# The normed input of a two-layer encoder moved by 32 bytes in its partitions

## The chip, the cores and the metric

The kernel runs on one core of a Trainium2 chip. The metric is the device time of one execution in microseconds (us); the time of a kernel is the median of several executions. In the profile the engines are PE (TensorE's matmuls), PEld (TensorE's loading of the stationary operand), DVE (VectorE), ACT (ScalarE), POOL (GpSimd) and SP (SyncE, which issues most DMAs).

## The reference

The kernel computes a small two-layer encoder for 256 tokens of width 2048 in float32, with 256 memory tokens beside them:

```python
m = rms_norm(mem, mem_norm)
h = x
for i in range(2):
    n = rms_norm(h, attn_norm[i])
    z = n @ (a_w_in if i == 0 else b_w_in)          # queries, keys, values, memory queries
    mix = neighbourhood_attention(...) if i == 0 else gqa_block_attention(...)
    km, vm = split(m @ w_mem_kv[i])
    cross = memory_attention(qm, km, vm)
    h = h + concatenate([mix, cross]) @ w_o[i]
    n = rms_norm(h, mlp_norm[i])
    h = h + square(relu(n @ w_up[i])) @ w_down[i]   # inner width 8192
return rms_norm(h, final_norm)
```

## The kernel before

**Split numbers.** Every float32 operand of a large product is split in two parts of a type that TensorE multiplies at full rate: hi, a rounded copy (ScalarE, line 299), and lo, the rest (VectorE, line 300). A product is then three matmuls: hi·hi, hi·lo and lo·hi. The activations lie split in SBUF; the weights stream from memory in chunks of 1 MB (128 partitions of 2048 floats), are split in halves of 1024 columns, and are used once.

**Operands.** In each matmul one operand moves through the array (512 or 256 columns here) and the other is stationary (128 columns); the profile writes out<-moving,stationary or the other way round, whichever the program names first. Four helpers issue nearly all matmuls:

- `m_products` (lines 205, 208, 209): the weights (hi, lo, or uh, ul, or th, tl) move with 512 columns, a block of 128 tokens of the activations (nT, memT, cat or a_p) is stationary. It forms the values, the second layer's whole input projection, the output projections and the last eighth of the MLP's second product.
- `s_products` (lines 218 and 221): 128 columns of the weights are stationary, the activations (memT or nT) move, 512 columns with hi and 256 with lo, two of each in turn. It forms the memory keys and the first layer's queries and keys.
- `u_products` (lines 670 to 672): the MLP's first product; the weights uh and ul are stationary, hT moves with 256 columns.
- the second product's `run` (lines 779 to 781): the weights (bh, bl, then th, tl) move with 512 columns, a_s is stationary; the products are named p1 to p7, by the sums and differences of a seven-product scheme.

**Order.** The memory's keys and values come first, then the first layer's input projection with its attention beside it, its output projection and its MLP, and the same for the second layer. In the MLP, 56 times per layer, 48 matmuls of ps_u alternate with 21 of p (9 with bh and bl, 12 with th and tl). A hand-made list of steps, each with loading, preparing and running parts, sets the order on all engines; data that an engine waits for is prepared some steps ahead.

**Where the tiles lie.** Tiles are taken from pools, and pools are stacked in each partition of SBUF: const, keep and small on the left, behind them ring and cat (in the attention stages) or mlp (in the MLP); on the right, from the other end downwards, work (attention) or side (MLP). Tiles and pools are rounded to 32 bytes and not further. `wide` (line 418) takes a tile of 32768 bytes in keep, which holds four things in turn: nT0, the first layer's normed input (taken in `x_norm`, line 531); hT0, the MLP's input (in `guard`, line 605); nT1, the second layer's normed input (in `down_done`, line 917); hT1; at the end a row of gains (line 899). In the program before it begins at byte 34464, which is 32 past a multiple of 64 (and of 128). Counted from the sizes, the others begin at:

| tiles | pool | bytes past a multiple of 128 |
|---|---|---|
| nT0, hT0, nT1, hT1 | keep, tag wide | 32 |
| raw, hi, lo | ring | 0 |
| memT, cat | cat | 0 |
| z, c, a_s, a_p, bh, bl, th, tl | mlp | 0 |
| raw_U, uh, ul, b, t, raw_T | side | 96 |
| qT, kT, km, sc, pT, va, vb, vm | work | 96 |

Slices of these tiles begin at whole multiples of 64 bytes from the tile's start (512 bytes for 128 columns).

Of the kernel before, what the change touches and what calls it, by code (L numbers as in the profile page):

```python
# [11 lines left out]
F32R = mybir.dt.float32r  # L12
# [5 lines left out]
P = 128  # L18
# [3 lines left out]
KT = D // P  # L22
# [48 lines left out]
def encoder_kernel(ctx: ExitStack, tc: tile.TileContext, t: dict, out: bass.AP):  # L71
# [4 lines left out]
    def opened(name, side="left", space=None, bufs=1):  # L76
        kw = {"space": space} if space else {}
        manager = tc.tile_pool(name=name, bufs=bufs, side=side, reuse_waits="tile", **kw)
        pools[name] = manager, manager.__enter__()
        return pools[name][1]  # L80

    def closed(*names):
        for name in names:
            pools.pop(name)[0].__exit__(None, None, None)

    const = opened("const")
    keep = opened("keep")
# [11 lines left out]
    def open_ring():  # L99
        at.ring = opened("ring")  # L100
        at.cat = opened("cat")
# [84 lines left out]
    def later(n, fn, *args):  # L186
        pending.append((state["tick"] + n, fn, args))
# [133 lines left out]
    def split_pair(dst, src, which, k):  # L321

        g = gain(which, k)
        nc.scalar.activation(dst[:, k, :SEQ], src, AF.Copy, scale=g)
        nc.vector.scalar_tensor_tensor(dst[:, k, SEQ:], src, g, dst[:, k, :SEQ].bitcast(F32),  # L325
                                       op0=ALU.mult, op1=ALU.subtract)
# [88 lines left out]
    def get(name):  # L415
        return lambda: box[name]

    def wide(name):
        return keep.tile([P, KT, 512], F32R, tag="wide", name=name)

    def keys(name):
        return at.work.tile([P, NMH, 512], F32R, tag="keys", bufs=1, name=name)
# [105 lines left out]

    def x_norm(j):
        if j == 0:  # L530
            box["nT"] = wide("nT0")
        for k in (2 * j, 2 * j + 1):
            split_pair(box["nT"], box["xT"][k // 8][:, k % 8, :], G_A0, k)

# [49 lines left out]
    def sum_squares(which, i, nb):  # L584
        sq = at.side.tile([P, 512], BF16, tag="junk", bufs=2, name="sq")
        nc.scalar.activation(sq, h[:, i, nb * 512 : (nb + 1) * 512], AF.Square,
                             accum_out=ssq[which][:, i, nb : nb + 1])

    def mean_square(which, n, name):

        s = small.tile([P, NT], F32, tag="ss0", name="ss_t")
        nc.vector.tensor_reduce(s, ssq[which][:, :, :n], axis=AX.X, op=ALU.add)
        v = keep.tile([P, NT], F32, tag=name, name=name)
        nc.vector.tensor_scalar(v, s, 1.0 / (n * 512), EPS, op0=ALU.mult, op1=ALU.add)
        return v

    def o_done(layer, nb):
        which = 2 * layer

        def guard():  # L600

            box["near"] = mean_square(which, GUARD, "near")
            box["scale"] = keep.tile([P, NT], F32, tag="scale", name="scale")
            nc.gpsimd.tensor_tensor(box["scale"], box["near"], mhalf[:, :NT], op=ALU.pow)
            box["hT"] = wide(f"hT{layer}")
# [195 lines left out]
    def add_scaled(hs, src, factor):  # L801
        nc.vector.scalar_tensor_tensor(hs, src, factor, hs, op0=ALU.mult, op1=ALU.add)
# [104 lines left out]
    def down_done(layer, nb):  # L907
        def f(w):
            for i in range(NT):
                add_scaled(h[:, i, nb * 512 : (nb + 1) * 512], w.ps[i], box["inv"][:, i : i + 1])  # L910
            for i in range(NT):
                sum_squares(2 * layer + 1, i, nb)
            if layer == 1:
                later(1, times_gf, nb)
                return
            if nb == 0:
                box["nT"] = wide("nT1")
            later(1, transposed, box["nT"], lambda i, k: h[:, i, k * P : (k + 1) * P],
                  list(range(nb * 4, nb * 4 + 4)), G_A1)
            if nb == 3:  # L920
                closed("mlp")
                open_ring()

                def norm():
                    box["rstd"] = keep.tile([P, NT], F32, name="rstd1")
                    v = mean_square(1, 4, "full")
                    nc.gpsimd.tensor_tensor(box["rstd"], v, mhalf[:, :NT], op=ALU.pow)
                later(2, norm)
        return f
# [145 lines left out]
    for j in range(8):  # L1075
        later(24 + j, x_norm, j)
# [122 lines left out]
```

## Time and profile before

| | |
|---|---|
| median of 3 executions | 2070.88 us (2068.25 to 2073.3) |
| the profiled execution | 2069.22 us |
| its span, first to last instruction | 2067.2 us |
| mean granted TensorE clock | 0.997 of full speed |
| ACT busy | 1251.3 us (61%) |
| DMA | 433.78 MB, 210 GB/s on average |

The span is what the page's shares refer to; the profiled execution's time has some 2 us around it. The page lists the busy time of each engine, then the chain of work that ended last, then the costliest groups of instructions with the mean duration of one. Durations of matmuls overlap, since one begins before the one before has drained, so a row's mean is no rate: rates come from start times, in the timeline or in the windows view, which gives busy time, instruction counts (those still running at the stretch's start included), clock and DMA share for chosen stretches of the span.

### The profile page before, as it was taken

The page shows a single profiled execution, that of the slowest core. Times are in us where ns is not written, and L with a number is a line of the kernel's source. Part 1 is how long each engine was busy: PE and PEld are TensorE (multiplying, and loading weights), DVE is VectorE, ACT ScalarE, POOL GpSimd, SP SyncE. Part 2 cuts the span into 40 slices and gives each one's busy share as a digit, 9 for nine tenths or more (in the row PEclk, how much of TensorE's full clock was granted, in tenths as well). Part 3 has the DMA queues.
Part 4 walks back from the last instruction along what each step waited for, and adds up shares of the span by engine and source line. Part 5 has one row for each costly group of instructions (what it writes and reads, how often), then busy time and mean ns, then how long its engine had stood idle before and what let it go on. Part 6 is the DMA issues. An engine that isn't in the chain of part 4 may idle for free.

```text
span 2067.2 us, 31544 instructions
## 1 busy us (share of the span) xinstructions
PE 2039.7 (99%) x12516; PEld 1815.0 (88%) x12516; DVE 1668.6 (81%) x2047; ACT 1251.3 (61%) x1642; POOL 119.2 (6%) x144
## 2 busy tenths in 40 slices
PE   8999999999999999999999999999999999999998
PEld 6888888889999999999988888889999999999996
DVE  6767667566899999999996667666988999999896
ACT  6755555555666666666656557555666666666653
POOL 0000000000010000010000001000000000000000
PEclk9999999999999999999999999999999999999999
DMA  7755555736777787787765454536877787777773
GB/s 266 297 183 177 189 175 170 274 105 202 223 235 231 218 240 225 225 240 226 231 201 209 171 177 143 188 138 197 232 227 227 224 242 222 233 232 223 232 225 121
DMA packets 92996, 433.78 MB, mean 210 GB/s; under 512 B 10416, under 2 KB 12080, under 8 KB 59568
## 3 DMA queue, kind: packets, MB, share of 16 engines
q1 hardware_dynamic: 75456, 399.25, 57.3%
q0 software_dynamic: 16816, 31.46, 8.6%
q8 instruction: 98, 1.61, 0.3%
q10 hardware_dynamic: 576, 1.05, 0.1%
q14 instruction: 50, 0.41, 0.1%
HBM read 398.17 MB, written 4.19 MB: 195 GB/s over the span
## 4 chain that ended last, share of the span: by engine, by line
PE 97%; DVE 1%; issue 1%; DMA 1%; ACT 0%; SPq 0%; POOLq 0%; POOL 0%; DVEq 0%; ACTq 0%
PE ps_u L672 11%; PE ps_u L670 11%; PE ps_u L671 11%; PE p L779 9%; PE p L780 9%; PE p L781 9%; PE ps_m L205 8%; PE ps_m L208 8%; PE ps_m L209 8%; PE ps_s L218 7%; PE ps_s L221 3%; PE pt_a L379 1%; PE pt_n L317 0%; PE av L387 0%; PE sc_ps L353 0%
## 5 line engine op out<-in xcount | busy, mean ns | idle before, releaser
L671 PE MATMUL ps_u<-hT,uh 128*128 128x256 f32 x2048 | 569.3, 278 | 3.7 <-DVE hT L325 3.6
L670 PE MATMUL ps_u<-hT,uh 128*128 128x256 f32 x2048 | 569.9, 278 | 1.5 <-ACT uh L299 1.5
L672 PE MATMUL ps_u<-hT,ul 128*128 128x256 f32 x2048 | 569.3, 278 | 1.5 <-DVE ul L300 1.3
L299 ACT ACTIVATE uh<-raw_U 128x1024 fp32r<-128x1024 f32 x278 | 295.0, 1062 | 325.2 <-PE ps_u L671 301.9
L300 DVE TENSOR_TENSOR lo<-raw,hi 128x1024 fp32r<-128x1024 f32 (+1 forms) x222 | 266.3, 1204 | 167.7 <-ACT hi L299 166.4
L671 PEld LDWEIGHTS ps_u<-hT,uh 128*128 128x128 f32 x2048 | 385.9, 188 | 9.1 <-DVE hT L325 4.5
L670 PEld LDWEIGHTS ps_u<-hT,uh 128*128 128x128 f32 x2048 | 386.3, 189 | 7.6 <-ACT uh L299 1.9
L672 PEld LDWEIGHTS ps_u<-hT,ul 128*128 128x128 f32 x2048 | 387.1, 189 | 3.0 <-DVE ul L300 2.3
L300 DVE TENSOR_TENSOR ul<-raw_U,uh 128x1024 fp32r<-128x1024 f32 x278 | 337.9, 1219 | 35.4 <-ACT uh L299 35.4
L299 ACT ACTIVATE hi<-raw 128x1024 fp32r<-128x1024 f32 (+1 forms) x222 | 231.3, 1047 | 218.7 <-PE ps_m L209 116.1
L299 ACT ACTIVATE th<-t 128x2048 fp32r<-128x2048 f32 x112 | 215.2, 1921 | 124.9 <-PE p L781 118.2
L300 DVE TENSOR_TENSOR tl<-t,th 128x2048 fp32r<-128x2048 f32 x112 | 256.3, 2288 | 40.3 <-ACT th L299 39.9
L300 DVE TENSOR_TENSOR bl<-b,bh 128x1536 fp32r<-128x1536 f32 x112 | 196.1, 1751 | 0.4
L780 PE MATMUL p<-tl,a_s 128*128 128x512 f32 x448 | 177.2, 396 | 0.0
L781 PE MATMUL p<-th,a_s 128*128 128x512 f32 x448 | 174.4, 389 | 0.0
L299 ACT ACTIVATE bh<-b 128x1536 fp32r<-128x1536 f32 x112 | 166.2, 1484 | 6.4
L779 PE MATMUL p<-th,a_s 128*128 128x512 f32 x448 | 166.1, 395 | 0.0
L759 POOL DMA_DIRECT2D t<-b x112 | 97.0, 866 | 1168.3 <-DVE t L758 377.5
L218 PE MATMUL ps_s<-nT,hi 128*128 128x512 f32 x448 | 141.7, 394 | 0.0
L781 PE MATMUL p<-bh,a_s 128*128 128x512 f32 x336 | 131.1, 390 | 0.0
L780 PE MATMUL p<-bl,a_s 128*128 128x512 f32 x336 | 130.9, 390 | 0.0
L758 DVE TENSOR_TENSOR t<-t,b 128x512 f32<-128x512 f32 x112 | 77.2, 690 | 48.2 <-DMA t<-in_w_pair 36.4
(235 smaller groups left out, 3510.6 us busy)
## 6 DMA issues: line engine op xcount, KB each, us to landing
raw_U<-in_w_up SPq DMA_DIRECT2D x128, 1024.0 KB, 6.6
b<-in_w_pair SPq DMA_DIRECT2D x112, 768.0 KB, 4.5
raw<-in_w_o SPq DMA_DIRECT2D x32, 1024.0 KB, 5.0
t<-in_w_pair SPq DMA_DIRECT2D x112, 256.0 KB, 3.4
t<-b POOLq DMA_DIRECT2D x112, 256.0 KB, 6.6
raw<-in_w_b SPq DMA_DIRECT2D x21, 1024.0 KB, 5.0
raw<-in_w_av SPq DMA_DIRECT2D x12, 1024.0 KB, 4.9
raw<-in_w_aq SPq DMA_DIRECT2D x12, 1024.0 KB, 4.9
```

Of the source, the lines that this page charges most:

```text
L205: first = nc.tensor.matmul(w.ps[i], ah, hi[:, s], start=st, stop=False)
L208: nc.tensor.matmul(w.ps[i], ah, lo[:, s], start=False, stop=False)
L209: nc.tensor.matmul(w.ps[i], al, hi[:, s], start=False, stop=sp)
L218: nc.tensor.matmul(ps, hi[:, s], acts[:, k0 + j, :], start=k0 + j == 0, stop=False)
L299: nc.scalar.activation(dst_hi, src, AF.Copy)
L300: nc.vector.tensor_tensor(dst_lo, src, dst_hi.bitcast(F32), op=ALU.subtract)
L670: nc.tensor.matmul(ps, hi[:, s], acts[:, k, :SEQ], start=k == 0, stop=False)
L671: nc.tensor.matmul(ps, hi[:, s], acts[:, k, SEQ:], start=False, stop=False)
L672: nc.tensor.matmul(ps, lo[:, s], acts[:, k, :SEQ], start=False, stop=k == KT - 1)
L779: nc.tensor.matmul(ps, a[:, 0, ai, :], hi[:, s], start=begins, stop=False)
L780: nc.tensor.matmul(ps, a[:, 0, ai, :], lo[:, s], start=False, stop=False)
L781: nc.tensor.matmul(ps, a[:, 1, ai, :], hi[:, s], start=False, stop=ends)
```

## The change

`wide` gets a parameter, shift. Its tile now has room for 8 more floats (32800 bytes in place of 32768), and what it returns is a view of the old size that begins `shift` floats into it. The two normed inputs nT0 and nT1 ask for a shift of 8 floats, 32 bytes; hT0 and hT1 ask for none. So nT begins at byte 34496, a multiple of 64, and hT at 34464 as before.

```diff
-    def wide(name):
-        return keep.tile([P, KT, 512], F32R, tag="wide", name=name)
+    def wide(name, shift=0):
+        room = keep.tile([P, KT * 512 + 8], F32R, tag="wide", name=name)
+        return room[:, shift : shift + KT * 512].rearrange("p (a b) -> p a b", b=512)
...
     def x_norm(j):
         if j == 0:
-            box["nT"] = wide("nT0")
+            box["nT"] = wide("nT0", 8)
...
             if nb == 0:
-                box["nT"] = wide("nT1")
+                box["nT"] = wide("nT1", 8)
```

The tile itself is 32 bytes longer, and the left pools are stacked behind it.

## The prediction

> **What bounds the kernel now.** I read the page first: the span, the busy times and the chain that ended last.
>
> ```profile
> span 2067.2 us, 31544 instructions
> ...
> PE 2039.7 (99%) x12516; PEld 1815.0 (88%) x12516; DVE 1668.6 (81%) x2047; ACT 1251.3 (61%) x1642; POOL 119.2 (6%) x144
> ...
> PE 97%; DVE 1%; issue 1%; DMA 1%; ACT 0%; SPq 0%; POOLq 0%; POOL 0%; DVEq 0%; ACTq 0%
> PE ps_u L672 11%; PE ps_u L670 11%; PE ps_u L671 11%; PE p L779 9%; PE p L780 9%; PE p L781 9%; PE ps_m L205 8%; PE ps_m L208 8%; PE ps_m L209 8%; PE ps_s L218 7%; PE ps_s L221 3%; PE pt_a L379 1%; PE pt_n L317 0%; PE av L387 0%; PE sc_ps L353 0%
> ```
>
> TensorE is busy for 99% of the span and is 97% of the chain. So the time is the sum of the intervals from one matmul's start to the next, and a change of addresses counts if it changes such an interval. A matmul's duration in the trace (388 ns) is latency, since they overlap; the interval must be taken from starts. So next the timeline, in two stretches that run the same code (line 205 to 209, moving tile hi or lo) with different stationary tiles.
>
> ```profile
> 392.24 0.39 PE L208 MATMUL ps_m<-lo,cat 128*128 128x512 f32 x1
> ...
> 395.87 0.39 PE L205 MATMUL ps_m<-hi,cat 128*128 128x512 f32 x1
> ```
>
> ```profile
> 1238.08 0.40 PE L208 MATMUL ps_m<-lo,nT 128*128 128x512 f32 x1
> ...
> 1241.81 0.40 PE L209 MATMUL ps_m<-hi,nT 128*128 128x512 f32 x1
> ```
>
> Both have 16 steps. With cat a step takes 3.63/16 = 226.9 ns, with nT 3.73/16 = 233.1 ns. Shape, moving tile and line are the same; the stationary tile's address is not: cat begins at a multiple of 64 bytes, nT 32 past one. Below I call the first **even** and the second **odd**. The windows view gives such stretches for every pair of kinds, and its clock column shows 1.00 in all of them, so no throttle explains them. Columns: stretch, length, busy time and matmuls begun or still running, clock, DMA share, GB/s.
>
> ```profile
> core 0: us, PE busy (x), PEclk, DMA share, GB/s
> 392.24:395.87 3.63, 3.63 (x17) 1.00 1.01 414
> 1238.08:1241.81 3.73, 3.73 (x18) 1.00 0.37 154
> 1076.75:1079.56 2.81, 2.81 (x14) 1.00 0.25 105
> 1125.80:1127.40 1.60, 1.60 (x8) 1.00 1.00 420
> 1307.26:1308.94 1.68, 1.68 (x17) 1.00 0.63 190
> 529.33:531.60 2.27, 2.27 (x23) 1.00 1.00 325
> 717.11:719.58 2.47, 2.47 (x23) 1.00 0.96 232
> 518.32:523.79 5.47, 5.47 (x49) 1.00 0.59 218
> 523.79:528.62 4.83, 4.83 (x24) 1.00 0.77 202
> 158.25:158.94 0.69, 0.69 (x6) 1.00 0.71 297
> ```
>
> Steps counted in the timeline as above, the rows from the third on give:
> - uh with a_p, odd moving and even stationary, 512 columns: 12 steps, 2.81/12 = 234.2 ns.
> - uh with nT, both odd, 512 columns: 7 steps, 228.6 ns.
> - attention scores and values (sc_ps, av), both odd, 256 columns: 14 steps, 120.0 ns.
> - ps_u (hT with uh), both odd, 256 columns: 20 steps, 113.5 ns; in another group 21 steps, 117.6 ns.
> - a whole MLP group of 48 ps_u: 5.47 us, 114.0 ns each. The group of 21 p behind it (both even, 512 columns): 4.83 us, 230.0 ns each, so above the 226.9 of cat: after each change of kind the intervals take some ten matmuls to come down.
> - four ps_s with nT (two of 512 columns, two of 256): 0.69 us.
>
> Thus mixed parity costs 6 to 7 ns per matmul, both even nothing, and both odd anything from nothing (113.5 = half of 226.9) to 6.5 ns (120.0). The DMA share goes from 0.25 to 1.01 and does not order them.
>
> At this place the Trainium skill, "TensorE: Matmul & The Clock Gate", section "Step-by-step: what each phase is for", speaks against any effect: TensorE has two independent SBUF read ports, one for the moving and one for the stationary operand. The trace does not bear that out as far as speed goes (226.9 against 233.1 ns); by the rule the sum would be nothing.
>
> **What the change does, part by part.** No instruction, DMA, wait or queue is added or moved. It moves addresses, and more than it names. nT becomes even. The tile of tag wide grows by 32 bytes, though, and all that is allocated behind it on the left side (small, then ring with raw, hi, lo and cat with memT and cat, or mlp with bh, bl, th, tl, a_s, a_p, c, z) moves 32 bytes with it: even becomes odd. hT stays odd, and the right side (work, side: uh, ul, raw_U, t, qT, kT) stays odd.
>
> ACT, DVE and the DMAs first. ACT and DVE already do the same work to odd and even tiles:
>
> ```profile
> L299 ACT ACTIVATE uh<-raw_U x278: 1042/1062/1069, 391.6 to 2040.6; 128x1024 fp32r<-128x1024 f32 x139
> L299 ACT ACTIVATE hi<-raw x222: 614/1061/1222, 6.4 to 1372.0; 128x1024 fp32r<-128x1024 f32 x107, 128x512 fp32r<-128x512 f32 x4
> ```
>
> ```profile
> L300 DVE TENSOR_TENSOR ul<-raw_U,uh x278: 1209/1218/1227, 392.9 to 2041.7; 128x1024 fp32r<-128x1024 f32 x139
> L300 DVE TENSOR_TENSOR lo<-raw,hi x222: 682/1225/1227, 7.0 to 1373.2; 128x1024 fp32r<-128x1024 f32 x107, 128x512 fp32r<-128x512 f32 x4
> ```
>
> Medians (middle number) 1062 odd against 1061 even, and 1218 against 1225: nothing. What hides a small change of theirs is slack on DVE, as 17 alternations of the MLP (ps_u and p groups) show; the columns are the stretch, its length and the busy times of PE, PEld, DVE, ACT and POOL:
>
> ```profile
> 520.73:695.83 175.10, 175.10 (x1175) 160.17 (x1174) 159.11 (x170) 115.36 (x118) 14.80 (x17) 1.00 0.78 229
> ```
>
> DVE works 159.11 of 175.10 us. If its operations became over 10% longer that cover would be gone, and each alternation would last as long as DVE's work.
>
> The TensorE counts come from the source view (count behind each x; two moving, hi and lo, make three matmuls per product, so the rows of line 205 stand for three times as many):
>
> ```profile
> L205 PE MATMUL ps_m<-hi,nT x264: 389/396/486, 125.1 to 1273.0; 128*128 128x512 f32 x132
> L205 PE MATMUL ps_m<-hi,cat x256: 387/389/501, 350.4 to 1382.6; 128*128 128x512 f32 x128
> L205 PE MATMUL ps_m<-hi,memT x64: 387/389/397, 31.7 to 100.6; 128*128 128x512 f32 x64
> L205 PE MATMUL ps_m<-uh,a_p x64: 388/396/502, 1074.0 to 2055.1; 128*128 128x512 f32 x64
> L205 PE MATMUL ps_m<-th,a_p x64: 387/389/398, 1080.7 to 2057.9; 128*128 128x512 f32 x64
> L205 PE MATMUL ps_m<-uh,nT x24: 387/394/399, 1117.1 to 1147.7; 128*128 128x512 f32 x24
> ```
>
> ```profile
> L779 PE MATMUL p<-th,a_s x448: 389/395/401, 503.2 to 2010.5; 128*128 128x512 f32 x150
> L779 PE MATMUL p<-bh,a_s x336: 387/389/401, 498.4 to 2000.7; 128*128 128x512 f32 x168
> ```
>
> ```profile
> L218 PE MATMUL ps_s<-nT,hi x448: 389/392/582, 101.3 to 349.9; 128*128 128x512 f32 x150
> ```
>
> One price is unknown: both odd at 512 columns in long rows. Its bounds are 226.9 ns (as ps_u at 113.5 has it) and 226.9 + 6.5 = 233.4 ns (the 6.5 that scores and values pay). Between lies 228.6, uh with nT, from 7 steps of a stage with 72 matmuls. I take **233.4**: the scores and values at 120.0 have both tiles at one offset (96 past a multiple of 128), as the moved tiles will have (32 past on both sides), whereas the fast ps_u pairs hT, 32 past, with uh, 96 past, and so does uh with nT. That is the choice on which the sign hangs.
>
> 1. hi with nT, 264 × 3 = 792: mixed before, mixed after (233.1 to 234.2 at most): 0, bounds 0 and 792 × 1.1 = 0.9 us.
> 2. uh with nT, 72: both odd to mixed, 72 × (234.2 − 228.6) = +0.4 us.
> 3. ps_s with nT, 448 × 2 = 896, groups of four: mixed before and after. 0; bounds from 4 clean ones (2 × 226.9 + 2 × 113.5 = 681 ns) to 707 ns, which adds to each of the four the 4.1 that ps_u pays in its slow groups: 224 × −9 to 224 × +17 ns, −2.0 to +3.8 us.
> 4. cat 768, memT 192, th with a_p 192, in all 1152, both even to both odd: 1152 × 6.5 = 7.5 us; a tenth of them follow a change of kind and are not clean today, so **+6.7**; bounds 0 and 7.5.
> 5. p, 112 × 21 = 2352, both even to both odd: 21 × 233.4 = 4.90 for 4.83 us, 112 × 0.07 = **+8.0**; lower bound 21 × 226.9 = 4.76, −7.8 us.
> 6. ps_u keeps its addresses, 48 per alternation. Clean it is 48 × 113.5 = 5.45, so 0.02 of its 5.47 is coming down after p. Behind a p of its own parity this may go, at most 112 × 0.02 = −2.4 us; I take half, −1.2.
> 7. uh with a_p, 192: mixed to both odd, by uh with nT: 192 × (228.6 − 234.2) = −1.1 us.
>
> Sum: 0.4 + 6.7 + 8.0 − 1.2 − 1.1 = +12.8 us. The profiled execution took 2069.22 us (the span 2067.2 and 2.0 around it), so 2082.0; it lies 1.7 below the median of 2070.88. On the median that is 2083.7, and I say 2083. Within the bounds of items 3 to 6 this forecast alone goes from 2076 to 2089.
>
> **The rivals.**
> *Equal parity is what counts* (faster). Both odd is as clean as both even, and a group that follows one of its own parity starts clean. Then an alternation is 48 × 113.5 + 21 × 226.9 = 10.21 us in place of 175.10/17 = 10.30: −0.09 × 112 = −10 us; uh with a_p gives 192 × −7.3 = −1.4, uh with nT +0.4. That is 2060. It decides if p behind ps_u runs at 227 from its first matmuls. For it speaks ps_u at 113.5; against it speak scores and values at 120.0, and the 117.6 that ps_u has at times. 0.15.
>
> *Both odd costs what uh with nT costs*, 228.6: p 21 × 228.6 = 4.80, −0.03 × 112 = −3.4; item 4 1152 × 1.7 × 0.9 = +1.8; items 2, 6 and 7 stay; −3.5, so 2067. For it: the only row of that shape. Against: seven steps. 0.13.
>
> *ps_u falls into its slow state behind the changed p.* It has the addresses it had, but 117.6 in some groups shows that what runs before decides. 48 × (117.6 − 113.5) = 0.20 us × 112 = +22 on top: 2105, or 2090 on the rival before. For it: the changed p no longer settles. Against: most groups of today come down behind a p of 230.0 on average. 0.12.
>
> *Addresses count for nothing and the difference between cat and nT has another cause*, such as what DMA writes meanwhile (shares 1.01 and 0.37, the slower one having less): 2071. 0.10. It is also what the Trainium skill, "SBUF — State Buffer", section "Specifications (TRN2)", suggests: 16-byte cachelines, of which 32 bytes are two whole ones; on that figure an estimate of the change is nothing, and the two stretches above do not agree with it.
>
> *The change does no more than it says* (what lies behind is rounded back to 64): only nT gets even. 792 × (226.9 − 233.1) = −4.9, ps_s −2.0, uh with nT +0.4: 2064. 0.05.
>
> **How the numbers follow.** The forecast has 0.45. The range 2058 to 2095 holds it and all rivals but the slow ps_u at 2105. A measurement of this kernel tells about 0.2%, 4.1 us, from no change. Faster: the first rival, the last, and some of the second, 0.23. Same: the rest of the second and the fourth, 0.20. Slower: forecast and slow ps_u, 0.57.
>
> **What would show it.** The same instructions in the same order, clock 1.00. In the timeline: hi with cat at 233 (item 4), not 227; p groups of 4.90 us, not 4.83 (item 5); ps_u groups no longer than 5.47, or 5.64 if the third rival is right; hi with nT still 233, which says that hi moved; uh with a_p below 234. Cat at 227 and p at 4.76 would mean that equal parity counts and I have the wrong sign; hi with nT at 227 and cat at 227 that nothing but nT moved.

## The result

| | before | changed |
|---|---|---|
| median of 6 executions | 2069.9 us (2068.25 to 2073.3) | 2083.41 us (2081.07 to 2088.6) |
| ratio to before, 95% interval | | 1.0064 (1.0054 to 1.0074) |
| profiled execution's span | 2067.2 us | 2081.0 us |

The changed kernel is 13.5 us slower. Its page, the span, the busy times and the end of the chain of waits:

```profile
span 2081.0 us, 31544 instructions
...
PE 2053.4 (99%) x12516; PEld 1833.4 (88%) x12516; DVE 1670.8 (80%) x2047; ACT 1249.8 (60%) x1642; POOL 119.2 (6%) x144
...
PE 97%; DVE 1%; issue 1%; DMA 1%; ACT 0%; SPq 0%; POOLq 0%; POOL 0%; DVEq 0%; ACTq 0%
PE ps_u L673 12%; PE ps_u L671 11%; PE ps_u L672 11%; PE p L780 9%; PE p L781 9%; PE p L782 9%; PE ps_m L205 8%; PE ps_m L208 8%; PE ps_m L209 8%; PE ps_s L218 6%; PE ps_s L221 3%; PE pt_a L379 1%; PE pt_n L317 0%; PE sc_ps L354 0%; PE av L387 0%
```

The counts are those of before, and TensorE still has 97% of the chain. ACT and DVE are within 3 us of before. Only ps_u has a larger share. The windows view of TensorE in the changed kernel, with stretches like those of before: one group of 48 ps_u, the 21 p behind it, 17 such alternations, 16 steps of hi with cat, 16 of hi with nT (stretch, length, busy time and matmuls, clock, DMA share, GB/s):

```profile
518.05:523.70 5.65, 5.65 (x49) 1.00 0.50 190
523.70:528.49 4.79, 4.79 (x24) 1.00 0.90 230
518.05:695.53 177.48, 177.48 (x1175) 1.00 0.77 226
391.16:394.79 3.63, 3.63 (x18) 1.00 1.00 409
1244.07:1247.79 3.72, 3.72 (x17) 1.00 0.37 156
```

The reader is to see three things. First, hi with cat still takes 3.63 us in 16 steps, 226.9 ns each, though both tiles are odd now: the cost that the prediction put there isn't there. Second, the 21 p are not slower but faster, 4.79 for 4.83 us. Third, all the loss is in ps_u, whose addresses did not change: 5.65 for 5.47 us. The 17 alternations went from 175.10 to 177.48 us, 0.14 each, 15.7 us in 112. (112 is the count of p divided by 21. The trace has 96 whole alternations of 48 and 21; in the others ps_u and p are split into shorter stretches, and 816 matmuls of ps_u run ahead of the first p of their layer.)

The same for the whole trace: for each matmul the time to the next one's start, waits included, summed by kind.

| kind | matmuls | before, us | changed, us | difference |
|---|---|---|---|---|
| ps_u, hT with uh and ul | 6144 | 716.3 | 734.9 | +18.6 |
| p | 2352 | 540.7 | 537.0 | −3.8 |
| uh with a_p | 192 | 46.5 | 45.8 | −0.7 |
| uh with nT | 72 | 16.75 | 16.96 | +0.2 |
| hi with nT | 792 | 185.9 | 185.9 | 0.0 |
| hi with cat, hi with memT | 960 | 220.5 | 220.5 | −0.1 |
| th with a_p | 192 | 45.3 | 45.3 | 0.0 |
| ps_s with nT | 896 | 157.2 | 157.2 | 0.0 |

Of the +18.6 us of ps_u, 17.0 lie in the 96 whole groups of 48 and 1.5 in the two stretches of 372 matmuls that run ahead of the first p of a layer.

In two places the trace of the changed kernel shows what kind of loss it is. First, in the last alternations of a layer a single pair of p (x2 in one row) stands between two stretches of ps_u. The timeline, with the first and last rows of each stretch (start, duration of one, or from the first's start to the last's end where a row stands for several):

```profile
1050.85 0.28 PE L673 MATMUL ps_u<-hT,ul 128*128 128x256 f32 x1
...
1053.56 0.28 PE L672 MATMUL ps_u<-hT,uh 128*128 128x256 f32 x1
1053.68 0.63 PE L780 MATMUL p<-th,a_s 128*128 128x512 f32 x2
1054.15 0.28 PE L673 MATMUL ps_u<-hT,ul 128*128 128x256 f32 x1
1054.27 0.28 PE L671 MATMUL ps_u<-hT,uh 128*128 128x256 f32 x1
...
1056.53 0.28 PE L673 MATMUL ps_u<-hT,ul 128*128 128x256 f32 x1
```

From 1050.85 to 1053.56 there are 23 steps: 117.8 ns each. From 1054.27 to 1056.53 there are 20: 113.0 ns. The tiles have the same offsets on both sides of the pair, 32 and 96 past a multiple of 128.

Second, the stretches of 372 at the start of a layer, where no p has run yet. Here are 200 steps of ps_u from the first layer and 200 from the second, in the windows view (stretch, length, busy times of PE, PEld, DVE, ACT and POOL, clock, DMA share, GB/s):

```profile
475.15:497.81 22.66, 22.66 (x202) 22.66 (x201) 14.50 (x21) 13.09 (x19) 0.00 (x0) 1.00 0.53 186
1421.17:1444.73 23.56, 23.56 (x203) 23.56 (x201) 14.54 (x21) 13.02 (x19) 0.00 (x0) 1.00 0.54 180
```

That is 113.3 ns each in the first layer and 117.8 in the second, with the same tiles, the same clock, the same DMA share within 0.01 and as much work of DVE and ACT within 0.1 us. So ps_u has (at least) two rates that hold themselves at one set of addresses. That what stands ahead of a stretch chooses between them is the theory that the experiments test. In the trace of before the groups of 48 came down to 113.5 within six matmuls; in the changed kernel they stay at 117.7.

### The profile page after: what moved, and what is told of

Same layout as the page of the kernel before. It is cut to its first block, busy times and chain, and to the rows that moved or that the text cites. A ratio compares the mean times of both kernels' runs of the same rounds, so it can differ in the third digit from the quotient of the medians.

```text
span 2081.0 us, 31544 instructions
## 1 busy us (share of the span) xinstructions
PE 2053.4 (99%) x12516; PEld 1833.4 (88%) x12516; DVE 1670.8 (80%) x2047; ACT 1249.8 (60%) x1642; POOL 119.2 (6%) x144
## 4 chain that ended last, share of the span: by engine, by line
PE 97%; DVE 1%; issue 1%; DMA 1%; ACT 0%; SPq 0%; POOLq 0%; POOL 0%; DVEq 0%; ACTq 0%
PE ps_u L673 12%; PE ps_u L671 11%; PE ps_u L672 11%; PE p L780 9%; PE p L781 9%; PE p L782 9%; PE ps_m L205 8%; PE ps_m L208 8%; PE ps_m L209 8%; PE ps_s L218 6%; PE ps_s L221 3%; PE pt_a L379 1%; PE pt_n L317 0%; PE sc_ps L354 0%; PE av L387 0%
## 5 line engine op out<-in xcount | busy, mean ns | idle before, releaser
L672 PE MATMUL ps_u<-hT,uh 128*128 128x256 f32 x2048 | 576.5, 282 | 4.0 <-DVE hT L325 4.0
L671 PE MATMUL ps_u<-hT,uh 128*128 128x256 f32 x2048 | 576.9, 282 | 1.5 <-ACT uh L299 1.5
L673 PE MATMUL ps_u<-hT,ul 128*128 128x256 f32 x2048 | 576.8, 282 | 1.3 <-DVE ul L300 1.2
L782 PE MATMUL p<-bh,a_s 128*128 128x512 f32 x336 | 130.8, 389 | 0.0
L780 PE MATMUL p<-bh,a_s 128*128 128x512 f32 x336 | 108.2, 390 | 0.0
```

The source lines that it names most:

```text
L671: nc.tensor.matmul(ps, hi[:, s], acts[:, k, :SEQ], start=k == 0, stop=False)
L672: nc.tensor.matmul(ps, hi[:, s], acts[:, k, SEQ:], start=False, stop=False)
L673: nc.tensor.matmul(ps, lo[:, s], acts[:, k, :SEQ], start=False, stop=k == KT - 1)
L780: nc.tensor.matmul(ps, a[:, 0, ai, :], hi[:, s], start=begins, stop=False)
L782: nc.tensor.matmul(ps, a[:, 1, ai, :], hi[:, s], start=False, stop=ends)
```

## The experiments

Two theories were put against each other. **Entry**: the operands of p, which the change moves by 32 bytes, set how ps_u begins, and it holds the rate with which it begins. **Traffic**: ps_u is slow because ACT, DVE and DMAs now work on tiles at odd multiples of 32 while TensorE reads hT and uh, odd themselves. Beside these stood the question what parity costs at all. Every kernel was timed against the kernel before in the same session. The edits of size alone, nT alone, the cuts, all even, nT even with the MLP by 128, and the change with the MLP by 128 are shown against the changed kernel, the others against the kernel before.

| kernel | MLP's operands moved by | ps_u, 48 | p, 21 | 17 alternations | median, us | ratio to before (95%) |
|---|---|---|---|---|---|---|
| before | 0 | 5.47 | 4.83 | 175.10 | 2069.9 | |
| the change | 32 | 5.65 | 4.79 | 177.48 | 2083.41 | 1.0064 (1.0054 to 1.0074) |
| size alone | 32 | 5.65 | 4.79 | 177.48 | 2079.81 | 1.0041 (1.0026 to 1.0056) |
| nT alone | 64 | 5.65 | 4.82 | 178.05 | 2082.85 | 1.0057 (1.0042 to 1.0072) |
| MLP alone | 32 | 5.65 | 4.79 | 177.48 | 2082.24 | 1.0054 (1.0039 to 1.0069) |
| ring and cat alone | 0 | 5.48 | 4.82 | 175.10 | 2066.31 | 0.9980 (0.9970 to 0.9990) |
| z and c alone | 128 | 5.46 | 4.79 | 174.31 | 2063.61 | 0.9967 (0.9955 to 0.9979) |
| the change, two cuts | 32 | 5.84 | 4.79 | 180.65 | 2107.51 | 1.0177 (1.0157 to 1.0196) |
| MLP by 96 | 96 | 5.65 | 4.76 | 177.03 | 2078.23 | 1.0037 (1.0025 to 1.0049) |
| all even | 64 | 5.75 | 4.79 | 179.18 | 2091.73 | 1.0103 (1.0087 to 1.0120) |
| MLP by 128 | 128 | 5.46 | 4.79 | 174.31 | 2064.98 | 0.9978 (0.9968 to 0.9987) |
| nT even, MLP by 128 | 128 | 5.46 | 4.79 | 174.31 | 2061.28 | 0.9953 (0.9939 to 0.9967) |
| ring odd, MLP by 224 | 224 | 5.66 | 4.78 | 177.48 | 2076.56 | 1.0033 (1.0020 to 1.0047) |
| the change, MLP by 128 | 128 | 5.46 | 4.79 | 174.31 | 2064.81 | 0.9975 (0.9964 to 0.9985) |

### Which of the moved tiles costs

**Size alone.** The tile grows, nothing in it is shifted.

```diff
-            box["nT"] = wide("nT0", 8)
+            box["nT"] = wide("nT0")
...
-                box["nT"] = wide("nT1", 8)
+                box["nT"] = wide("nT1")
```

> The tile of tag wide is 32 bytes longer and nothing is shifted in it: nT stays 32 past a multiple of 64, all left tiles behind it move as in the change. If equal parity of the two operands is what a matmul's interval hangs on, hi with nT (792) falls from 233 to 227, 4.9 us, and ps_s with nT by 0 to 2: 2077 to 2079 us, with the groups of 48 ps_u at 5.65 us as in the change. If nT's own offset were what costs, hi with nT stays at 233 and the time is that of the change, 2083.

Measured 2079.81, 3.6 less than the change and a little above the expected 2077 to 2079. hi with nT, now both odd, in 16 steps (windows view of TensorE):

```profile
1242.90:1246.54 3.64, 3.64 (x17) 1.00 0.38 158
```

227.5 ns in place of 233. Over the trace hi with nT falls by 4.1 us (181.9 for 185.9); the expected 4.9 counted every one as settled. ps_u is at 5.65: shifting nT has no part in the loss, it only takes a gain away.

**nT alone.** The tile has 16 floats more in place of 8.

```diff
-        room = keep.tile([P, KT * 512 + 8], F32R, tag="wide", name=name)
+        room = keep.tile([P, KT * 512 + 16], F32R, tag="wide", name=name)
```

> The tile is 64 bytes longer, so that what lies behind it keeps its offset to 64, and nT alone gets even. By equal parity hi with nT falls from 233 to 227 (-4.9 us), ps_s by 0 to 2, uh with nT rises by 0.2 to 0.4; ps_u 5.47 and p 4.82 us per group as before: 2063 to 2065. If it is the move of nT that slows ps_u, the time is 2078 to 2083.

It came out at 2082.85, against what I expected of parity. The windows of this kernel (ps_u, p, hi with nT):

```profile
518.01:523.66 5.65, 5.65 (x49) 1.00 0.50 191
523.66:528.48 4.82, 4.82 (x23) 1.00 0.91 232
...
1243.85:1247.48 3.63, 3.63 (x17) 1.00 0.36 153
```

hi with nT, both even, is at 226.9 as expected (−4.1 us in all). But ps_u stuck, though no tile of the MLP changed its parity to 64: they lie 64 bytes further. So the parity of p is not what chooses ps_u's rate; the offset counts more finely than that. (That it isn't nT's own move is shown further down, by the run with nT even and the MLP by 128.)

**MLP alone**, with nT, ring and cat as before, by 32 bytes at the head of the pool:

```diff
                 at.mlp = opened("mlp")
+                at.mlp.tile([P, 8], F32, tag="pad", name="pad")
```

> Only the tiles of the pool mlp (z, c, a_s, a_p, bh, bl, th, tl) move by 32 bytes; nT, ring and cat lie as before. If the loss comes from the MLP's pool alone, ps_u groups 5.65 and p groups 4.79 us, uh with a_p 0.7 us less in all: 2069.9 + 112 x (0.18 - 0.03) - 0.7 = 2086 at most, 2083 by the sums of the trace. If ring or cat has a part in it, under 2080.

2082.24, ps_u and p as in the change:

```profile
519.01:524.66 5.65, 5.65 (x50) 1.00 0.47 184
524.66:529.45 4.79, 4.79 (x24) 1.00 0.81 231
```

The MLP's pool carries the whole loss.

**Ring and cat alone**, the same pad at the head of the ring:

```diff
         at.ring = opened("ring")
+        at.ring.tile([P, 8], F32, tag="pad", name="pad")
```

> Only raw, hi, lo, memT and cat move by 32 bytes; nT and the MLP's tiles lie as before. By equal parity hi with nT is at 227 (-4.9 us), cat and memT stay at 227; ps_u changes only in the two groups that follow cat (+0.2 us): 2064 to 2066. If both-odd operands cost by themselves, as the prediction had it, cat and memT rise to 233 and the time to 2071 or more.

2066.31, faster than before. The alternations, hi with cat (both odd) and hi with nT (both odd):

```profile
519.55:694.65 175.10, 175.10 (x1175) 1.00 0.77 229
391.18:394.80 3.62, 3.62 (x17) 1.00 1.01 388
1243.34:1246.99 3.65, 3.65 (x17) 1.00 0.51 211
```

Both odd is as clean as both even for 512 columns: 226.3 ns for cat, which within the rounding of 0.01 us to a stretch is the 226.9 of before, and, with a trace of settling, 228.1 for nT. The prediction's price of 233.4 falls here.

### Entry or traffic

**z and c alone.** These two are read and written by ACT and DVE only. The operands of p were to keep their offset within 128, so 96 bytes more follow c, and they lie 128 bytes further.

```diff
+                at.mlp.tile([P, 8], F32, tag="pad", name="pad")
                 box["z"] = [at.mlp.tile([P, 4, 512], F32, tag=f"z{q}", name=f"z{q}") for q in range(2)]
...
+            if part == 0 and m == 1:
+                at.mlp.tile([P, 24], F32, tag="pad2", name="pad2")
             a = at.mlp.tile([P, 2, 7, P], F32R, tag="a", bufs=6, name="a_s")
```

> Of the MLP's tiles z and c alone, which TensorE never reads, move by 32 bytes; a_s, bh, bl, th and tl move by 128, so that they keep their offset. If ps_u is slow because ACT and DVE work on tiles 32 past a multiple of 64 beside it, ps_u groups go towards 5.65 us and the time above 2075. If what decides is the run of matmuls ahead of ps_u, nothing changes: 5.47 us, 2068 to 2072.

2063.61: neither theory's number. Traffic fails (ps_u is not slower), but the time isn't that of before either:

```profile
518.98:524.44 5.46, 5.46 (x49) 1.00 0.57 212
524.44:529.23 4.79, 4.79 (x23) 1.00 0.84 219
```

Both groups settle sooner than before. Either z and c do better at odd offsets, or the 128 bytes matter. The next kernel moves all by 128, z and c too:

```diff
+                at.mlp.tile([P, 32], F32, tag="pad", name="pad")
                 box["z"] = [at.mlp.tile([P, 4, 512], F32, tag=f"z{q}", name=f"z{q}") for q in range(2)]
```

> All of the MLP's tiles move by 128 bytes, z and c with them: a_s, bh, bl, th and tl lie exactly as in the run with z and c 32 past, and z and c are even again. If that run was faster because the operands of p moved by 128, this one is as fast: ps_u groups 5.46 us, 2062 to 2065. If it was faster because z and c were odd, this one is as before: 5.477 us, 2068 to 2072.

2064.98, and the same groups:

```profile
518.35:523.81 5.46, 5.46 (x50) 1.00 0.56 218
523.81:528.60 4.79, 4.79 (x24) 1.00 0.87 227
```

So the offset of z and c is nothing, and what counts is where the operands of p lie; a move by a whole 128 bytes counts too. That fits entry. Traffic from odd tiles has no run left that speaks for it: with nT alone all of the MLP's moved tiles are even, and ps_u sticks. No run moves where TensorE reads the operands of p without moving where ACT and DVE write them; that it is TensorE's own history rests on the two places in the changed kernel's trace and on the next run.

**Cuts in the changed kernel.** If the entry chooses, a disturbance inside a group should be able to throw ps_u over, as the pair of p did.

```diff
-            nc.tensor.matmul(ps, hi[:, s], acts[:, k, SEQ:], start=False, stop=False)
+            cut = {10: P, 13: 64}.get(k, SEQ)
+            nc.tensor.matmul(ps[:, :cut], hi[:, s], acts[:, k, SEQ : SEQ + cut], start=False, stop=False)
+            if cut < SEQ:
+                nc.tensor.matmul(ps[:, cut:], hi[:, s], acts[:, k, SEQ + cut :], start=False, stop=False)
```

> The changed kernel, with two matmuls in each group of 48 ps_u cut in two parts by columns (128 and 128 at k = 10, 64 and 192 at k = 13): 224 matmuls more, no address altered. If ps_u has two rates that hold themselves and the entry chooses, a cut can throw it over: 113.5 ns per matmul behind one of the cuts, 36 to 42 x 4.1 ns x 112 = 17 to 19 us less, and a cut costs 0 to 57 ns (half an interval), 0 to 13 us in all: 2065 to 2079. If the addresses or the traffic of the other engines hold ps_u at 117.6, it stays there behind both cuts and the time is 2083 to 2096.

2107.51, dearer than either theory said, and I had misplaced the cuts: in a group of 48 the half with k from 8 on comes second, so little of the group lies behind them. (The kernel also has 256 matmuls more, not 224, since the groups outside the alternations are cut as well.) The 31 steps of one group ahead of its first cut:

```profile
522.46:526.11 3.65, 3.65 (x33) 1.00 0.59 236
```

They take 117.7 ns each. The timeline around the second cut of this group:

```profile
527.15 0.28 PE L671 MATMUL ps_u<-hT,uh 128*128 128x256 f32 x1
527.26 0.19 PE L673 MATMUL ps_u<-hT,uh 128*128 128x64 f32 x1
527.29 0.33 PE L675 MATMUL ps_u<-hT,uh 128*128 128x192 f32 x1
527.46 0.31 PE L676 MATMUL ps_u<-hT,ul 128*128 128x256 f32 x1
527.60 0.28 PE L671 MATMUL ps_u<-hT,uh 128*128 128x256 f32 x1
...
527.96 0.28 PE L671 MATMUL ps_u<-hT,uh 128*128 128x256 f32 x1
528.07 0.28 PE L673 MATMUL ps_u<-hT,uh 128*128 128x256 f32 x1
528.18 0.28 PE L676 MATMUL ps_u<-hT,ul 128*128 128x256 f32 x1
528.30 0.40 PE L783 MATMUL p<-th,a_s 128*128 128x512 f32 x1
```

From 527.26 to 527.60 it is 0.34 us for what are two intervals of 0.12: a cut costs 0.1 us, twice what I had allowed. Behind it ps_u does come down, 0.34/3 = 113 ns from 527.96 to the end. Three intervals are few in one group, but the trace has 106 groups like this one, each of 5.84 us: in all of them ps_u is at 117.7 or 117.8 ahead of the first cut, and the last three intervals ahead of the second cut and the last three of the group are at 113.3 to 113.7. No address differs from the changed kernel. So a disturbance within a group does throw ps_u over, as entry says; but the few matmuls behind the cuts gain less than the cuts cost, and so the time is longer.

### Other offsets

**MLP by 96** (a pad of 24 floats at the head of the pool).

> The MLP's tiles alone move by 96 bytes: odd as in the change, but the other odd offset within 128. If the parity of p to 64 decides how ps_u begins, ps_u groups take 5.65 us and the time is 2082 to 2084, as with 32 bytes. If it is the exact offset, ps_u may begin well: ps_u 5.47 and p 4.79 give 2070 - 112 x 0.03 - 0.7 = 2066.

2078.23, lower than the one number and far above the other. ps_u and p:

```profile
519.90:525.55 5.65, 5.65 (x49) 1.00 0.52 199
525.55:530.31 4.76, 4.76 (x23) 1.00 0.91 232
```

ps_u sticks, but p begins clean, 4.76/21 = 226.7 ns from the first: the transition in one direction says nothing of the other.

**All even.** hT is shifted too, and 32 bytes at the end of the pool side bring uh and ul to even offsets; all the operands of the MLP then lie 64 past a multiple of 128.

```diff
-            box["hT"] = wide(f"hT{layer}")
+            box["hT"] = wide(f"hT{layer}", 8)
...
+            if part == 0 and n == 0:
+                at.side.tile([P, 8], F32, tag="pad", bufs=1, name="pad")
```

(and the tile of tag wide with 16 floats more).

> nT, hT and the pool side (uh, ul) lie at multiples of 64 too, so that every large matmul of the MLP and the projections has two even operands, all 64 past a multiple of 128. Equal parity gives hi with nT -4.9 us, uh with a_p and uh with nT together -1 to -2. If ps_u settles: 2062 to 2064, with p groups near 4.77 as much as 6 less. If ps_u needs a change of parity at its entry to come down, it sticks at 117.6: 2079 to 2082.

2091.73, 10 us above the higher of the two numbers and the slowest kernel without cuts:

```profile
520.82:526.57 5.75, 5.75 (x49) 1.00 0.48 181
```

5.75/48 is 119.8 ns, the 120.0 that scores and values have. ps_u's two tiles had been 32 and 96 past a multiple of 128; now both are 64 past one, as scores and values are both 96 past one. So the price of 6.5 ns that the prediction took from scores and values is real, but as far as these three pairs of offsets show it belongs to 256 columns with both operands at the same offset within 128, not to two odd ones, and not to 512 columns.

**Ring odd, MLP by 224** (pads of 8 floats in the ring and 56 in mlp): 96 past 128 as above, and 128 further.

> ring and cat 32 bytes further, nT as before, so both odd (hi with nT -4.1 us); the MLP's tiles 224 bytes further, 96 past a multiple of 128 as in the run with 96, and 128 more than there. p should begin at 227 right behind ps_u as it did at 96 (-6.4 us, p groups 4.77). ps_u is open: 5.46 us behind this p gives 2056, 5.65 gives 2077. A rule by the offset within 128 alone says 5.65.

2076.56: hi with nT gains 4.1 us, ps_u sticks, p settles in two matmuls rather than none.

```profile
516.52:522.18 5.66, 5.66 (x49) 1.00 0.52 197
522.18:526.96 4.78, 4.78 (x24) 1.00 0.76 216
```

### The loss undone

**nT even, MLP by 128**: the tile with 16 floats more, and 16 floats at the head of mlp.

```diff
-        room = keep.tile([P, KT * 512 + 8], F32R, tag="wide", name=name)
+        room = keep.tile([P, KT * 512 + 16], F32R, tag="wide", name=name)
...
+                at.mlp.tile([P, 16], F32, tag="pad", name="pad")
```

> nT even as in the change; all behind it moves by 64 bytes and the MLP's pool by 64 more, 128 in all, so that the ring keeps its parity and the MLP lies as in the run before this one. If the loss of the run with nT alone (+12) was ps_u's entry behind p at 64, it is gone: hi with nT -4.1 us, the MLP as in the run before, 2059 to 2061. If moving nT itself costs the MLP, over 2075.

2061.28, faster than both kernels. ps_u, p, and hi with nT in 16 steps:

```profile
517.52:522.98 5.46, 5.46 (x49) 1.00 0.65 234
522.98:527.77 4.79, 4.79 (x23) 1.00 0.70 204
...
1238.83:1242.47 3.64, 3.64 (x17) 1.00 0.50 205
```

It differs from the run with nT alone (2082.85) in 64 bytes ahead of the MLP's tiles, and in nothing else: 21.6 us.

**The change, MLP by 128**: the change in full, and 24 floats at the head of mlp.

> The change in full, with 96 bytes more ahead of the MLP's tiles, so that these lie 128 further than before, as in the two runs that were faster; nT is even, ring and cat are odd as in the change. If all that the change costs is ps_u's entry behind the moved p, the cost is gone and p's and ps_u's gain of those runs is there: ps_u groups 5.46, hi with nT still 233, uh with nT +0.2, the two ps_u groups behind cat +0.2: 2064 to 2066. If ring and cat at an odd offset cost anything, more.

2064.81, within what was expected. What the change adds to ring, cat and nT is kept here, and the loss is gone:

```profile
521.05:526.51 5.46, 5.46 (x50) 1.00 0.54 213
526.51:531.30 4.79, 4.79 (x23) 1.00 0.70 204
```

## Why the prediction was right in its number and wrong in its reasons

The time, 2083.41, is what was forecast, 2083. That is luck: two terms that were too high by 18.5 us together (items 4 and 5) cancelled a third that was too low by 19.8 (item 6).

- **Item 1**, hi with nT, 0: held. Mixed before, mixed after, 185.9 us both times, and it falls by 4.1 us wherever the parities are equal, even or odd.
- **Item 2**, uh with nT, +0.4: +0.2.
- **Item 3**, ps_s with nT, 0: held.
- **Item 4**, cat, memT and th with a_p, +6.7: 0.0. This is the step that failed, "I take **233.4**": both odd at 512 columns costs 226.9, the lower bound. The row of scores and values, which I held to be the nearest, was of 256 columns, and the run with all even shows that it pays for an equal offset within 128, at that size.
- **Item 5**, p, +8.0: −3.8. The same failed step. At 226.9 p even gains, since it settles sooner behind ps_u (4.79 us); the lower bound was −7.8.
- **Item 6**, ps_u, −1.2: +18.6. This step failed too: "ps_u keeps its addresses", but not its rate. The bounds there (−2.4 to 0) left out what a rival of my own said.
- **Item 7**, uh with a_p, −1.1: −0.7.

What happened is parts of two rivals at once. *Equal parity is what counts* was right for cat and memT and for most of each group of p; but it wanted p clean from its first matmul behind ps_u, and p still takes five to settle, so it gained 3.8 us and not 7.8. *ps_u falls into its slow state behind the changed p* was right for ps_u, 5.65 us a group. They were priced at −10 and +22, together +12. I gave them 0.15 and 0.12 and priced the second on top of the forecast or of 228.6, never on top of the first. As written the two differ on ps_u (113.5 against 117.6), but nothing keeps a faster p from coming with a slower ps_u. The sign the prediction gave rested on the wrong choice; with 226.9 in items 4 and 5 and without the slow ps_u its sum is 0.4 + 0 − 7.8 − 1.2 − 1.1 = −9.7 us, the other sign. By the signs it named itself, cat at 227 and p near 4.76 meant just that.

The row for the rival of the slow ps_u was on the table: 21 steps of ps_u at 117.6 in the kernel before, beside 20 at 113.5 with the same tiles. Two rates at one set of addresses mean that the history decides, and then a change of the history (p's addresses) may choose anew in all groups at once. The argument against it, that most groups came down, only says what the old history did.

One sum of the prediction doesn't come out: 2076 as the lower end of its own bounds. Items 3 to 6 at their lower bounds give 0.4 − 2.0 + 0 − 7.8 − 2.4 − 1.1 = −12.9 us, which is 2058, the lower end of its whole range.

The rival *addresses count for nothing* is out: kernels that differ from before in offsets alone lie between 0.9953 and 1.0103 of it, with intervals of 0.0017 at most to each side. So is *the change does no more than it says*: hi moved, and hi with nT stayed at 233.

The Trainium skill, "TensorE: Matmul & The Clock Gate", section "Back-to-back issue gap", gives the distance of isolated matmuls as the columns over 2.4 plus about 2.5 ns, 216 for 512, with no term for an address. For a sustained stream of 512 columns it gives about 131 ns. No stretch here reaches either: the lowest are at 226 to 227, and the offsets move it to 234.

What stays open is how the entry chooses. With p's operands 0 or 128 bytes from where they lay, ps_u comes down; with 32, 64, 96 and 224 it sticks in the groups of 48. All six agree with "a multiple of 128 from its place", but 0 and 128 differ in how soon they settle (5.47 and 5.46, 4.83 and 4.79), so the rule, if there is one, looks further than 128 bytes. Six offsets against one place of hT and uh don't make it. Nor can offsets be the whole of it: ahead of the first p of a layer the changed kernel runs ps_u at 113.3 in one layer and 117.8 in the other. What in those starts chose is not shown.

## What to carry to other kernels

Ask of a padding or a shift what lies behind it in the pool: here the 32 bytes that were announced for one tile moved all the MLP's operands too, and those carried the whole loss, while the tile itself would have gained 4.1 us. Where a kernel is bound by TensorE, read the interval from start to start by pairs of tiles with their offsets in the partition, and if one pair shows two intervals in one trace, price the worse one for all of its matmuls as a case of its own, on top of every other case. Try a few offsets of each pool (a pad tile at its head) and time them: from 2061 to 2092 us the work was the same.

## What the hardware showed that was not expected

- For 512 columns of fp32r the interval is 226.9 ns when moving and stationary tile are both at a multiple of 64 or both 32 past one, and about 233 when one is and the other isn't.
- For 256 columns it is 113.3 to 113.5 ns at best; with both tiles at the same offset within 128 it held at 120.0 (both 96 past: scores and values; both 64 past: ps_u with all even).
- With hT 32 and uh 96 past a multiple of 128, ps_u holds 113.5 or 117.6 ns for whole groups, over 200 steps at a time (113.3 and 117.8 in the changed kernel's two layers), and two matmuls of another kind in between are enough to go from one to the other (1053.68 in the changed kernel).
- Moving the operands of the matmuls ahead by 64 bytes and no other operand of the MLP changed the alternation from 10.25 (174.31/17) to 10.47 us (178.05/17), at a granted clock of 1.00 both times.
